# A decoder layer in fp32: single transposes between half units, a shared ring of load buffers, and seven-product units moved within the down projection

## The chip, the cores and the metric

The kernel runs on one core of one Trainium2 chip. The metric is the device time of one execution in microseconds; the median of three runs before the change is 1808.32 us (1804.74 to 1811.37). Five engines work side by side, each through its own queue in order: TensorE (PE, with its weight loads shown as PEld), VectorE (DVE), ScalarE (ACT), GpSimd (POOL) and SyncE (SP), which here issues nearly all transfers from memory.

## The reference

One layer of a decoder for 256 tokens of width 2048, all in float32. Cut to what matters:

```
def swiglu(x, w_gate, w_up, w_down):
    return (jax.nn.silu(x @ w_gate) * (x @ w_up)) @ w_down        # d_ff 5632

x = layer_norm(ALPHA * x + 0.5 * swiglu(x, ffn1_w_gate, ffn1_w_up, ffn1_w_down), ln1_g, ln1_b)
(c_q, c_kv, k_rope, q, k_c, v_c, k_s, v_s, k_w, v_w, g) = split_cols(x @ w_in, IN_SIZES)
o_mla = mla_attention(...)      # 8 heads, low-rank queries and keys
o_nsa = nsa_attention(...)      # 8 heads, compressed, selected and window branches
mix = jnp.concatenate([o_mla, o_nsa], axis=-1) @ w_out
x = layer_norm(ALPHA * x + mix, ln2_g, ln2_b)
x = layer_norm(ALPHA * x + 0.5 * swiglu(x, ffn2_w_gate, ffn2_w_up, ffn2_w_down), ln3_g, ln3_b)
```

The two SwiGLU layers hold most of the matmuls: each reads three matrices of 2048 x 5632.

## The kernel before

**Products.** Every fp32 operand is split into a high part (a cast on ScalarE, L81) and the rest (a subtraction on VectorE, L82), and one product is three matmuls of 512 columns (`mm3`, L86 to L88): high by high, high by low, low by high. The weights are split on the chip, piece by piece, as they arrive.

**Two ways to multiply.** `gemm` takes one chunk of 512 output columns and walks the input in pieces of 256 rows; a piece is one load of 512 KB (`load`) and 12 matmuls, for two halves of the tokens. `gemm2` takes a pair of chunks; a unit is 256 input rows by 1024 columns, two loads, and eight products, 24 matmuls. For the units in a list (`seven`) it uses seven products in place of eight: VectorE makes four sums of weight blocks (L236 to L238, into the tiles `sum`), and sums of the activations must have been made before. Four more banks collect these products, and after the last such unit ScalarE and VectorE make four corner values from them (L254 to L258, in working tiles `w`), to which the ends of the other four banks are added (L266). `GATE7`, `UP7` and `DOWN7` are the lists.

**Order of a SwiGLU layer.** The eleven chunks of d_ff stand in groups of 4, 4 and 3. In a group, pairs of chunks are gated: gate weights, then up weights (`gemm2`, except that the first pair of a layer loads its gate weights by `gemm`). Then the group's rows go through `down`: two pairs of output chunks over the group's input rows. In the third group `down` uses four single chunks. `NW` (10) working tiles hold the gated rows; `NM` (14) tiles `m` hold sums of activations and attention operands.

**Transposes.** A gated row block (128 tokens by 512) has to be transposed for `down`: four transposes into one bank (`go`, L365), then a split into tiles `thi`, `tlo`; where `down` has seven-product units, sums of the rows are transposed too (`go2`, L375). These steps are generators that `spawn` puts in lanes and `tick` advances. TensorE and SP run in the order in which the program is written, and a tick is where a waiting step may put its instructions in. `gemm2` ticks twice after each unit; `gemm` twice after each piece. While a seven-product stretch needs all eight banks, `held` keeps the steps waiting. ScalarE, VectorE and GpSimd are ordered by a scheduler when the program is built.

**Buffers.** Loads go into five tiles `raw`, weight sums into three tiles `sum`, splits into six pairs `whi`, `wlo`; TensorE has eight banks. SP issues loads in order and waits where the next buffer is still in use.

Of the kernel before, what the change touches and what calls it, by code (L numbers as in the profile page):

```python
# [18 lines left out]
P = 128  # L19
# [14 lines left out]
O_CKV, O_KR, O_Q, O_KC, O_KS, O_KW, O_G = 512, 768, 832, 1856, 2368, 2880, 3392  # L34
KT = 2
HEAD, SPARE = 8, 2
NM = 14
NW = 10
GATE7, UP7 = (2, 4, 5), (1, 2, 4, 5)
DOWN7 = (((3, 5), (1, 3, 5)), ((3, 5), (1, 3, 5)), ((), ()))  # L40
DFF, DTR, DEV, DLN, DSM = 4, 7, 2, 4, 4


# [1 line left out]
def layer(ctx: ExitStack, tc: tile.TileContext, a: dict, out: bass.AP):  # L45
# [34 lines left out]
    def split(hi, lo, src):  # L80
        A.copy(hi, src)  # L81
        V.tensor_tensor(lo, src, f(hi), op=OP.subtract)  # L82

    def mm3(ps, x, wh, wl, first, last):
        xh, xl = x
        PE.matmul(ps, xh, wh, start=first, stop=False)  # L86
        PE.matmul(ps, xh, wl, start=False, stop=False)  # L87
        PE.matmul(ps, xl, wh, start=False, stop=last)  # L88
# [28 lines left out]
    def tick(n):  # L117
        for _ in range(n):
            now[0] += 1
            steps()  # L120

    def drain(*which):
        while any(q in lanes for q in which) if which else lanes:
            tick(1)

    def load(w, c, pc, spare=False):

        ap, pairs, n = w[:3]
        paired = len(w) > 3
        k0, kn = pc[0], len(pc)  # L130
        assert pc == list(range(k0, k0 + kn)) and k0 // KT == pc[-1] // KT
        r0 = (c * pairs + k0 // KT) * P
        raw = rawp.tile([P, KT, NCH], F32, name="raw")
        order = list(range(kn))
        if paired:

            r0 = (c // 2 * pairs + k0 // KT) * P
            src = w[3][r0:r0 + P].rearrange("p (i j n) -> p i j n", i=2, j=2)[:, :, c % 2, :]
            if c % 2:
                order = order[::-1]  # L140
            if kn < KT:
                at = k0 % KT if c % 2 == 0 else 1 - k0 % KT
                src = src[:, at:at + 1]
            nc.sync.dma_start(raw[:, :kn, :n], src)
        else:
            nc.sync.dma_start(raw[:, :kn, :n], ap[r0:r0 + P].rearrange("p (k n) -> p k n", k=KT)[:, k0 % KT:k0 % KT + kn])
        if spare:
            out = []
            for j in range(kn):
                hi, lo = (am(F32R).rearrange("p a b -> p (a b)")[:, :n] for _ in range(2))  # L150
                split(hi, lo, raw[:, j, :n])
                out.append((hi, lo))
            return [out[j] for j in order]
        hi = hip.tile([P, KT, NCH], F32R, name="whi")
        lo = lop.tile([P, KT, NCH], F32R, name="wlo")
        split(hi[:, :kn, :n], lo[:, :kn, :n], raw[:, :kn, :n])
        return [(hi[:, j, :n], lo[:, j, :n]) for j in order]
# [46 lines left out]
    def gemm2(x, xs, seven, w, cp, kps, finish, each=None):  # L204

        src, pairs = W2[w]
        B, todo = {}, []
        s_first, s_last = min(seven), max(seven)
        for i in kps:
            k, l = 2 * i, 2 * i + 1
            if i in seven:
                todo.append((i, [("p1", (k, 0), "kn"), ((0, 1), 3, "lm"), ((0, 0), (l, 0), "ln"), ("p5", 0, "t1"),
                                 ("p7", 2, "t3"), ("p6", 1, "t2"), ((1, 0), (l, 1), "t4")]))
            else:
                todo.append((i, [((t, j), (kk, t), name) for name, kk, j in  # L220
                                 (("kn", k, 0), ("lm", l, 1), ("ln", l, 0), ("km", k, 1)) for t in range(NT)]))
        first, last = {}, {}
        for i, ops in todo:
            for o, op in enumerate(ops):
                first.setdefault(op[0], (i, o))
                last[op[0]] = (i, o)
        rest = {}
        for i, ops in todo:
            r0 = (cp * pairs + i) * P
            a_, b_ = (rawp.tile([P, KT, NCH], F32, name="raw") for _ in range(2))  # L230
            for j, dst in enumerate((a_, b_)):
                nc.sync.dma_start(dst, src[r0:r0 + P, 2 * j * NCH:2 * (j + 1) * NCH].rearrange("p (k n) -> p k n", k=KT))
            parts = [(a_, ("kn", "lm"), 2), (b_, ("ln", "km"), 1 if i in seven else 2)]
            if i in seven:
                t13, t24 = (sump.tile([P, KT, NCH], F32, name="sum") for _ in range(2))
                V.tensor_tensor(t13, a_, b_[:, 1:2, :].broadcast_to([P, 2, NCH]), op=OP.add)  # L236
                V.tensor_tensor(t24[:, 0], t13[:, 0], a_[:, 1], op=OP.add)  # L237
                V.tensor_tensor(t24[:, 1], t24[:, 0], b_[:, 0], op=OP.add)  # L238
                parts += [(t13, ("t1", "t3"), 2), (t24, ("t2", "t4"), 2)]
            wt = {}  # L240
            for v, names, n in parts:
                hi = hip.tile([P, KT, NCH], F32R, name="whi")
                lw = lop.tile([P, KT, NCH], F32R, name="wlo")
                split(hi[:, :n], lw[:, :n], v[:, :n])
                for j in range(n):
                    wt[names[j]] = (hi[:, j], lw[:, j])
            for o, (b, xp, name) in enumerate(ops):
                if b not in B:
                    B[b] = new_bank()
                xp = sl(xs[i], xp) if isinstance(xp, int) else x(*xp)  # L250
                mm3(B[b], xp, *wt[name], first[b] == (i, o), last[b] == (i, o))
            if i == s_last:
                p1, q, u, z = (wk([P, NCH]) for _ in range(4))
                A.copy(p1, B["p1"])  # L254
                V.tensor_tensor(q, B["p6"], p1, op=OP.add)
                V.tensor_tensor(u, B["p7"], q, op=OP.add)
                V.tensor_tensor(q, B["p5"], q, op=OP.subtract)
                V.tensor_tensor(z, B["p5"], u, op=OP.subtract)  # L258
                rest = {(0, 0): p1, (0, 1): q, (1, 0): u, (1, 1): z}

            held[0] = s_first - 1 <= i <= s_last
            tick(2)
            if each:
                each(i)
        for b, r in rest.items():
            V.tensor_tensor(r, B[b], r, op=OP.add)  # L266
            finish(*b, r)
# [30 lines left out]

    def load_x(k, n=2):

        raw = rawp.tile([P, KT, NCH], F32, name="raw")
        nc.sync.dma_start(raw[:, :n, :S], a["xT"][k * P:(k + n) * P, :].rearrange("(k p) n -> p k n", p=P))
        for t in range(NT):
            if k % 4 == 0:
                xT[k // 4, t] = new_T()
            hi, lo = xT[k // 4, t]
            j = k % 4
            split(hi[:, j:j + n, :], lo[:, j:j + n, :], raw[:, :n, t * P:(t + 1) * P])
        if k // KT in UP7:
            xs0[k // KT] = parts(sums([raw[:, j, t * P:(t + 1) * P] for t in range(NT) for j in range(2)]))  # L310
# [34 lines left out]
    def ffn(name, x, xs, done, begin=None, after=None, late=()):  # L345
# [4 lines left out]
        for gi, grp in enumerate(groups):  # L350
# [4 lines left out]
            def up(c, t, h):  # L355

                hs[c, t] = h

                def go(c=c, t=t):
                    yield DFF  # L360
                    while held[0]:
                        yield 1
                    pt = new_bank().rearrange("p (a b) -> p a b", a=4)
                    for j in range(4):
                        PE.transpose(pt[:, j, :], hs[c, t][:, j * P:(j + 1) * P], ident)  # L365
                    hT[c, t] = new_T()
                    split(hT[c, t][0], hT[c, t][1], pt)

                def go2(i, s):
                    yield DFF  # L370
                    while held[0]:
                        yield 1
                    pt = new_bank().rearrange("p (a b) -> p a b", a=4)
                    for j in range(4):
                        PE.transpose(pt[:, j, :], s[:, j, :], ident)  # L375
                    hS[i] = parts(pt)

                spawn(go())
                if t:
                    for i in (2 * c, 2 * c + 1):  # L380
                        if i in seven[0] | seven[1]:
                            spawn(go2(i, sums([hs[c, u][:, (2 * (i % 2) + j) * P:(2 * (i % 2) + j + 1) * P]
                                               for u in range(NT) for j in range(2)])))
                steps()

            for c0 in grp[::2]:
# [430 lines left out]
    def compress(src, n):  # L817
# [26 lines left out]
        for m in range(2):  # L844
            PE.transpose(pt[:, m, :], hs[:, m * P:(m + 1) * P], ident)
        hid = att.tile([P, 2, 32], F32, name="hid", bufs=2)
        x = stat.tile([P, 2, 32], F32, name="gx")
        u = stat.tile([P, 2, 32], F32, name="gu")
        V.tensor_reduce(x, pt[:, 0:2, :].rearrange("p m (j c) -> p m c j", j=4), axis=AX.X, op=OP.add)
        V.tensor_tensor(u, x, x, op=OP.mult)  # L850
        V.tensor_tensor(u, u, x, op=OP.mult)
# [209 lines left out]
```

## Time and profile before

| what | value |
|---|---|
| median of three runs | 1808.32 us |
| the profiled execution | 1809.37 us, its span 1807.7 us |
| TensorE busy | 1770.5 us (98%), 8166 matmuls |
| VectorE busy | 1532.3 us (85%) |
| ScalarE busy | 975.7 us (54%) |
| moved by DMA | 350 MB, 194 GB/s over the span |

Times are microseconds from the span's start. The end of a matmul in the trace is modelled, and matmuls overlap, so a busy TensorE says little about its pace; the distance between starts does. A number in square brackets at a row's end is the idle time of the engine just before it and what ended it.

### The profile page before, as it was taken

The numbers are of one execution on the slowest core, as the hardware profiler recorded it, in microseconds if no ns is written. First come the engines' busy times: TensorE is split into PE (matmuls) and PEld (weight loads), VectorE is DVE, ScalarE is ACT, GpSimd is POOL, SyncE is SP. The second block draws the span as 40 slices with busy tenths as digits, with TensorE's granted clock in tenths as the row PEclk, the third lists the DMA queues.
The fourth block names the chain that finished last, engine by engine and source line by source line (L and its number), as shares of the span: only waits on it lengthen the run. The fifth ranks groups of instructions, "written<-read, shape, count | busy, mean of one in ns | idle before, by whom it ended". The sixth has DMA issues, their size and how long they took to land.

```text
span 1807.7 us, 22569 instructions
## 1 busy us (share of the span) xinstructions
PE 1770.5 (98%) x8166; PEld 1454.8 (80%) x8166; DVE 1532.3 (85%) x2019; ACT 975.7 (54%) x1285; POOL 17.4 (1%) x40
## 2 busy tenths in 40 slices
PE   7999999999999999999999999999999999999997
PEld 5887888888888888887787787878888888888886
DVE  6899899999889986766466678899999999889976
ACT  5556455565546554644455556556456565556541
POOL 0000000000000000000000000000000000000000
PEclk9999999999999999999999999999999999999999
DMA  7765565556465665565643445566655655555564
GB/s 252 248 209 195 183 214 201 197 186 207 167 209 203 197 219 191 167 199 194 235 142 117 129 166 170 198 191 206 219 188 202 205 184 202 191 201 204 196 222 139
DMA packets 112543, 350.01 MB, mean 194 GB/s; under 512 B 11168, under 2 KB 17584, under 8 KB 112432
## 3 DMA queue, kind: packets, MB, share of 16 engines
q1 hardware_dynamic: 111120, 344.37, 57.2%
q0 software_dynamic: 1312, 4.21, 0.9%
q8 instruction: 64, 1.05, 0.2%
q14 instruction: 47, 0.39, 0.1%
HBM read 346.44 MB, written 2.10 MB: 193 GB/s over the span
## 4 chain that ended last, share of the span: by engine, by line
PE 86%; DVE 8%; DMA 3%; issue 2%; ACT 2%; SPq 0%; DVEq 0%; POOL 0%; ACTq 0%; POOLq 0%
PE bank L86 27%; PE bank L88 27%; PE bank L87 27%; DVE wlo L82 3%; DMA raw<-in_ffn_w_gate 2%; ACT whi L81 1%; DMA raw<-in_ffn_w_up 1%; PE bank L910 1%; PE bank L365 1%; PE bank L900 1%; PE bank L754 1%; DVE sum L236 1%; DVE w L395 1%; PE bank L836 1%; DVE w L266 1%
## 5 line engine op out<-in xcount | busy, mean ns | idle before, releaser
L81 ACT CAST whi<-raw 128x1024 fp32r<-128x1024 f32 (+3 forms) x622 | 599.3, 982 | 496.3 <-PE bank L88 392.7
L82 DVE TENSOR_TENSOR wlo<-raw,whi 128x1024 fp32r<-128x1024 f32 (+3 forms) x622 | 694.0, 1130 | 153.0 <-ACT whi L81 151.9
L86 PE MATMUL bank<-whi,thi 128*128 128x512 f32 (+1 forms) x2026 | 794.2, 392 | 3.5 <-ACT whi L81 1.8
L87 PE MATMUL bank<-wlo,thi 128*128 128x512 f32 (+1 forms) x2026 | 786.6, 388 | 2.8 <-DVE wlo L82 2.8
L88 PE MATMUL bank<-whi,tlo 128*128 128x512 f32 (+1 forms) x2026 | 786.1, 388 | 0.1
L86 PEld LDWEIGHTS bank<-whi,thi 128*128 128x128 f32 x2026 | 381.2, 188 | 85.2 <-issue 4.5
L87 PEld LDWEIGHTS bank<-wlo,thi 128*128 128x128 f32 x2026 | 381.4, 188 | 79.8 <-DVE wlo L82 5.2
L88 PEld LDWEIGHTS bank<-whi,tlo 128*128 128x128 f32 x2026 | 381.0, 188 | 78.2 <-DVE tlo L82 0.5
L81 ACT CAST whi<-sum 128x1024 fp32r<-128x1024 f32 x184 | 191.5, 1053 | 196.6 <-PE bank L88 78.7
L82 DVE TENSOR_TENSOR wlo<-sum,whi 128x1024 fp32r<-128x1024 f32 x184 | 219.5, 1217 | 15.9 <-ACT whi L81 14.9
L87 PE MATMUL bank<-wlo,m 128*128 128x512 f32 x368 | 143.4, 390 | 1.2 <-DVE wlo L82 1.2
L88 PE MATMUL bank<-whi,m 128*128 128x512 f32 x368 | 143.2, 389 | 0.0
L86 PE MATMUL bank<-whi,m 128*128 128x512 f32 x368 | 143.2, 389 | 0.0
L236 DVE TENSOR_TENSOR sum<-raw 128x1024 f32<-128x1024 f32 x92 | 111.9, 1217 | 17.4 <-DMA raw<-in_ffn_w_gate 15.7
L87 PEld LDWEIGHTS bank<-wlo,m 128*128 128x128 f32 x368 | 69.1, 188 | 16.2 <-DVE wlo L82 2.0
L86 PEld LDWEIGHTS bank<-whi,m 128*128 128x128 f32 x368 | 69.1, 188 | 14.4
L88 PEld LDWEIGHTS bank<-whi,m 128*128 128x128 f32 x368 | 69.1, 188 | 14.3
L266 DVE TENSOR_TENSOR w<-bank,w 128x512 f32<-128x512 f32 x112 | 74.4, 684 | 3.5 <-PE bank L88 3.5
L237 DVE TENSOR_TENSOR sum<-sum,raw 128x512 f32<-128x512 f32 x92 | 62.9, 684 | 0.5
L238 DVE TENSOR_TENSOR sum<-sum,raw 128x512 f32<-128x512 f32 x92 | 62.9, 683 | 0.5
L82 DVE TENSOR_TENSOR tlo<-bank,thi 128x512 fp32r<-128x512 f32 (+1 forms) x56 | 34.0, 642 | 4.0 <-ACT thi L81 4.0
L81 ACT CAST thi<-bank 128x512 fp32r<-128x512 f32 (+1 forms) x56 | 28.6, 558 | 16.2 <-PE bank L365 10.0
(178 smaller groups left out, 880.6 us busy)
## 6 DMA issues: line engine op xcount, KB each, us to landing
raw<-in_ffn_w_down SPq DMA_DIRECT2D x176, 512.0 KB, 4.6
raw<-in_ffn_w_up SPq DMA_DIRECT2D x160, 512.0 KB, 4.8
raw<-in_ffn_w_gate SPq DMA_DIRECT2D x159, 512.0 KB, 4.6
raw<-in_w_in SPq DMA_DIRECT2D x48, 512.0 KB, 4.5
raw<-in_ffn_gu SPq DMA_DIRECT2D x32, 512.0 KB, 5.0
raw<-in_w_out SPq DMA_DIRECT2D x32, 512.0 KB, 3.3
raw<-in_nsa_cmp_w_k SPq DMA_DIRECT2D x8, 512.0 KB, 3.7
raw<-in_nsa_cmp_w_v SPq DMA_DIRECT2D x8, 512.0 KB, 3.4
```

What stands on the lines that cost most here:

```text
L81: A.copy(hi, src)
L82: V.tensor_tensor(lo, src, f(hi), op=OP.subtract)
L86: PE.matmul(ps, xh, wh, start=first, stop=False)
L87: PE.matmul(ps, xh, wl, start=False, stop=False)
L88: PE.matmul(ps, xl, wh, start=False, stop=last)
L236: V.tensor_tensor(t13, a_, b_[:, 1:2, :].broadcast_to([P, 2, NCH]), op=OP.add)
L237: V.tensor_tensor(t24[:, 0], t13[:, 0], a_[:, 1], op=OP.add)
L238: V.tensor_tensor(t24[:, 1], t24[:, 0], b_[:, 0], op=OP.add)
L266: V.tensor_tensor(r, B[b], r, op=OP.add)
L365: PE.transpose(pt[:, j, :], hs[c, t][:, j * P:(j + 1) * P], ident)
L395: V.tensor_tensor(h, r, h, op=OP.mult)
L754: PE.matmul(o, qrT[t][:, hh, :], krT[:, b, :], start=False, stop=True)
```

## The change

Four edits. `go` and `go2` all go into one lane, "T", and take one tick each, so that at most one set of four transposes follows a tick; `gemm2` ticks once in the middle of a unit (after its fourth operation) and once at its end. The lists of `down`: the first chunk pair has no seven-product unit any more and is done by single chunks with `gemm`; the second has the units 1, 2, 4 and 5 (before: 3 and 5, and 1, 3 and 5). Plain loads and the loads of x take their buffer from `new_raw`, which goes round five `raw` and three `sum` tiles. The pools: 16 tiles `m` (14), 9 working tiles (10), two tiles each for `gx` and `gu` (three).

```
-NM = 14
-NW = 10
+NM = 16
+NW = 9
 GATE7, UP7 = (2, 4, 5), (1, 2, 4, 5)
-DOWN7 = (((3, 5), (1, 3, 5)), ((3, 5), (1, 3, 5)), ((), ()))
+DOWN7 = (((), (1, 2, 4, 5)), ((), (1, 2, 4, 5)), ((), ()))
...
+    turn = [0]
+
+    def new_raw():
+
+        turn[0] += 1
+        return (sump if turn[0] % 8 >= 5 else rawp).tile([P, KT, NCH], F32, name="sum" if turn[0] % 8 >= 5 else "raw")
+
     def load(w, c, pc, spare=False):
...
-        raw = rawp.tile([P, KT, NCH], F32, name="raw")
+        raw = new_raw()
...
                 mm3(B[b], xp, *wt[name], first[b] == (i, o), last[b] == (i, o))
+                if o == 3:
+                    tick(1)
...
             held[0] = s_first - 1 <= i <= s_last
-            tick(2)
+            tick(1)
...
+                ready = now[0] + DFF
+
                 def go(c=c, t=t):
-                    yield DFF
-                    while held[0]:
+                    while held[0] or now[0] < ready:
                         yield 1
                     pt = new_bank().rearrange("p (a b) -> p a b", a=4)
                     for j in range(4):
                         PE.transpose(pt[:, j, :], hs[c, t][:, j * P:(j + 1) * P], ident)
                     hT[c, t] = new_T()
                     split(hT[c, t][0], hT[c, t][1], pt)
+                    yield 1
...
-                spawn(go())
+                spawn(go(), "T")
...
                             spawn(go2(i, sums([hs[c, u][:, (2 * (i % 2) + j) * P:(2 * (i % 2) + j + 1) * P]
-                                               for u in range(NT) for j in range(2)])))
+                                               for u in range(NT) for j in range(2)])), "T")
```

`go2` changes as `go` does, and `load_x` as `load`. The change adds lines, so that an instruction's line after it is higher: L365 becomes L375, L375 becomes L385, L258 becomes L267, L266 becomes L275.

On TensorE, in the second gate stage of the first layer, the transposes stand before the change in one place, at the end of the seventh unit:

```order
L86 MATMUL bank<-whi,thi 128x512
L87 MATMUL bank<-wlo,thi 128x512
L88 MATMUL bank<-whi,tlo 128x512
L365 MATMUL bank<-ident,w 128x128 x12
L375 MATMUL bank<-ident,w 128x128 x4
L365 MATMUL bank<-ident,w 128x128 x4
L375 MATMUL bank<-ident,w 128x128 x4
L86 MATMUL bank<-whi,thi 128x512
```

After the change the same place holds the first four, and the next four stand 12 matmuls later (four products of three):

```order
L88 MATMUL bank<-whi,tlo 128x512
L375 MATMUL bank<-ident,w 128x128 x4
L86 MATMUL bank<-whi,thi 128x512
L87 MATMUL bank<-wlo,thi 128x512
L88 MATMUL bank<-whi,tlo 128x512
```

The other sets follow in the same way, one at the end of the stage, one in the first unit of the up stage, and the last two at the up stage's end. In the first down chunk two sets stand together after a piece (x8).

On SP, the first loads of the program, with the semaphores that each waits for; before the change the sixth is the first that waits for VectorE:

```order
L302 DMA raw<-in_xT 128x2x256
L144 DMA raw<-in_ffn_w_gate 128x2x512 [waits DMAHW0_49,DVE_49]
L302 DMA raw<-in_xT 128x2x256 [waits DMAHW1_49,DVE_49]
L144 DMA raw<-in_ffn_w_gate 128x2x512 [waits DMAHW2_49,DVE_49]
L302 DMA raw<-in_xT 128x2x256 [waits DMAHW3_49,DVE_49]
```

After it, from the same load on:

```order
L311 DMA sum<-in_xT 128x2x256
L151 DMA sum<-in_ffn_w_gate 128x2x512
L311 DMA sum<-in_xT 128x2x256
L151 DMA raw<-in_ffn_w_gate 128x2x512
L311 DMA raw<-in_xT 128x2x256 [waits DMAHW0_49,DVE_49]
```

The order of the loads is the same; the ninth is now the first that waits.

On VectorE, the corner values of that gate stage (L255 to L258) and what follows, before the change:

```order
L257 TENSOR_TENSOR w<-bank,w 128x512
L258 TENSOR_TENSOR w<-bank,w 128x512
L236 TENSOR_TENSOR sum<-raw 128x1024
L82 TENSOR_TENSOR wlo<-raw,whi 128x1024
L82 TENSOR_TENSOR tlo<-bank,thi 128x512 x3
L82 TENSOR_TENSOR m<-bank,m 128x512
L82 TENSOR_TENSOR tlo<-bank,thi 128x512
L82 TENSOR_TENSOR m<-bank,m 128x512
```

And after it:

```order
L266 TENSOR_TENSOR w<-bank,w 128x512
L243 TENSOR_TENSOR sum<-raw 128x1024
L82 TENSOR_TENSOR wlo<-raw,whi 128x1024
L267 TENSOR_TENSOR w<-bank,w 128x512
L82 TENSOR_TENSOR tlo<-bank,thi 128x512
L244 TENSOR_TENSOR sum<-sum,raw 128x512
```

The fourth corner value moved behind a weight sum and a weight split, and the splits of the transposed sets no longer stand together.

## Rows read from the trace of the kernel before

**Rows 1.** The page, busy time: engine, us, share of the span, instructions.

```profile
PE 1770.5 (98%) x8166; PEld 1454.8 (80%) x8166; DVE 1532.3 (85%) x2019; ACT 975.7 (54%) x1285; POOL 17.4 (1%) x40
```

**Rows 2.** TensorE's waits: for whom, us in total, times, longest.

```profile
PE bank L365 <- DVE tlo L82: 9.4, 8, 1.9
PE bank L86 <- ACT m L81: 7.4, 2, 5.3
PE bank L87 <- DVE wlo L82: 4.1, 6, 1.2
```

**Rows 3.** Stretches by stage: us, busy PE, PEld, DVE, ACT, POOL, clock, DMA, GB/s.

```profile
100.30:146.80 46.50, 44.55 (x209) 36.89 (x208) 45.78 (x63) 25.57 (x31) 0.00 (x0) 1.00 0.56 183
187.60:233.50 45.90, 44.60 (x208) 37.05 (x207) 40.10 (x51) 22.46 (x26) 0.00 (x0) 1.00 0.54 176
233.50:275.00 41.50, 41.50 (x185) 34.37 (x184) 37.65 (x43) 22.25 (x23) 0.00 (x0) 1.00 0.61 206
357.20:402.70 45.50, 44.61 (x209) 36.92 (x208) 44.97 (x61) 25.70 (x31) 0.00 (x0) 1.00 0.56 187
...
655.70:723.60 67.90, 67.67 (x309) 55.94 (x307) 45.93 (x58) 32.21 (x39) 0.56 (x1) 1.00 0.59 192
...
1174.80:1222.40 47.60, 45.05 (x208) 36.72 (x207) 45.98 (x64) 24.06 (x30) 2.73 (x5) 1.00 0.62 192
1222.40:1263.20 40.80, 40.80 (x181) 33.78 (x180) 40.57 (x46) 25.12 (x29) 0.00 (x0) 1.00 0.62 202
1263.20:1308.50 45.30, 44.60 (x207) 37.03 (x206) 44.99 (x60) 21.89 (x26) 1.62 (x3) 1.00 0.66 222
1432.30:1477.40 45.10, 44.45 (x208) 36.87 (x207) 44.34 (x60) 25.61 (x31) 0.00 (x0) 1.00 0.56 187
```

**Rows 4.** Timeline of TensorE around one burst: start, us, operation, idle before.

```profile
135.21 0.39 PE L87 MATMUL bank<-wlo,thi 128*128 128x512 f32 x1
...
136.12 0.39 PE L88 MATMUL bank<-whi,tlo 128*128 128x512 f32 x1
...
140.20 0.66 PE L365 MATMUL bank<-ident,w 128*128 128x128 f32 x4 [1.95 <-DVE tlo L82]
...
142.00 0.40 PE L86 MATMUL bank<-whi,thi 128*128 128x512 f32 x1
```

**Rows 5.** Timeline of TensorE around a set of four transposes alone.

```profile
718.89 0.39 PE L88 MATMUL bank<-whi,tlo 128*128 128x512 f32 x1
...
720.26 0.40 PE L86 MATMUL bank<-whi,thi 128*128 128x512 f32 x1
```

**Rows 6.** The start: stretches, TensorE's first matmuls and its pause, an SP wait.

```profile
5.30:35.50 30.20, 25.98 (x96) 19.05 (x96) 21.36 (x47) 17.98 (x33) 0.00 (x0) 1.00 0.82 274
35.50:59.50 24.00, 23.76 (x96) 19.29 (x97) 18.20 (x18) 12.83 (x14) 0.00 (x0) 0.93 0.85 292
...
30.00:35.00 5.00, 2.95 (x12) 1.99 (x11) 1.19 (x2) 2.55 (x4) 0.00 (x0) 1.00 1.01 358
35.00:40.00 5.00, 4.26 (x12) 3.20 (x13) 4.04 (x4) 4.87 (x7) 0.00 (x0) 0.74 0.69 234
...
8.30 0.63 PE L86 MATMUL bank<-whi,thi 128*128 128x512 f32 x1
8.73 0.63 PE L87 MATMUL bank<-wlo,thi 128*128 128x512 f32 x1
...
35.51 0.50 PE L86 MATMUL bank<-m,thi 128*128 128x512 f32 x1 [2.17 <-ACT m L81]
...
SPq L144 <- DVE tlo L82: 7.0, 5, 2.8
```

**Rows 7.** Timeline of TensorE at a wait in the stretch from 1174.80.

```profile
1190.69 0.50 PE L87 MATMUL bank<-wlo,m 128*128 128x512 f32 x1 [1.23 <-DVE wlo L82]
```

**Rows 8.** Groups of instructions: count, busy us, mean ns, idle before.

```profile
L375 PE MATMUL bank<-ident,w 128*128 128x128 f32 x48 | 7.4, 277 | 0.0
L258 DVE TENSOR_TENSOR w<-bank,w 128x512 f32<-128x512 f32 x28 | 19.0, 678 | 0.0
```

More of the change, by code (lines that the diff above doesn't have):

```diff
@@ L299, in load_x @@
     def load_x(k, n=2):
-        raw = rawp.tile([P, KT, NCH], F32, name="raw")
+        raw = new_raw()
         nc.sync.dma_start(raw[:, :n, :S], a["xT"][k * P:(k + n) * P, :].rearrange("(k p) n -> p k n", p=P))
@@ L367, in go @@
                     split(hT[c, t][0], hT[c, t][1], pt)
+                    yield 1
                 def go2(i, s):
-                    yield DFF
-                    while held[0]:
+                    while held[0] or now[0] < ready:
                         yield 1
@@ L376, in go2 @@
                     hS[i] = parts(pt)
-                spawn(go())
+                    yield 1
+                spawn(go(), "T")
                 if t:
@@ L846, in compress @@
         hid = att.tile([P, 2, 32], F32, name="hid", bufs=2)
-        x = stat.tile([P, 2, 32], F32, name="gx")
-        u = stat.tile([P, 2, 32], F32, name="gu")
+        x = stat.tile([P, 2, 32], F32, name="gx", bufs=2)
+        u = stat.tile([P, 2, 32], F32, name="gu", bufs=2)
         V.tensor_reduce(x, pt[:, 0:2, :].rearrange("p m (j c) -> p m c j", j=4), axis=AX.X, op=OP.add)
```

## The prediction

> **What bounds the kernel now.** I read the busy shares first. TensorE is busy for 98% of the span, VectorE for 85% [rows 1]: what the kernel can win is in TensorE's pauses and in its count of instructions. Second, the waits of TensorE [rows 2]: the longest sum, 9.4 us in 8 waits, is the transposes of the SwiGLU rows (L365) waiting for the VectorE half of a split (L82), which frees a bank. The second, 7.4 us in 2 waits, is the start of the program, where a split waits for a weight that has not landed.
>
> Third, the stretches stage by stage, cut at the first matmul of each stage [rows 3]. The pitch of a matmul is 0.227 us (four from 135.21 to 136.12 [rows 4]), and a stage of 183 matmuls without transposes lasts 41.50 us = 183 x 0.227: nothing but pitch. Eight stages are longer: four of gate weights (46.50, 45.50, 47.60, 45.10; 183 matmuls each) and four of down's first chunk pair (45.90, 45.30 and two like the first of these; 186 each, so 42.18 without transposes). Together 367.7 us against 4 x 41.50 + 4 x 42.18 = 334.7: 33 us over. 1.5 of it is another wait, in the stretch at 1174.80: 1.23 us for a split that VectorE reaches late [rows 7], with the slower pitch behind it. The other 31.5 us are 176 transposes in eight bursts. In one burst (24 transposes, 136.12 to 142.00) the pause is 1.95 us: the fifth set of four finds no free bank [rows 4].
>
> The start: two stages of 96 matmuls (21.8 us of pitch each) last 30.20 and 24.00 us [rows 6], 10.6 us over.
>
> **The change part by part.**
>
> *One set of transposes per half unit.* It removes the eight bursts. How much does a set of four cost alone? From the matmul at 718.89 to that at 720.26 are 1.37 us, which hold four matmuls (0.91) and one set: 0.46 us [rows 5]. The order after the change has 48 sets in the two groups concerned (44 before; the L375 row counts 12 sums rows in 48 transposes [rows 8], and the new list of units makes 16), with 12 matmuls between most of them and pairs of sets in the first down chunk. 48 x 0.46 = 22.1 us, against 31.5: **-9.4 us**. In the third groups two runs of 16 and 8 become six sets: +0.1 us each, +0.2.
>
> What hides the splits of a set? Each needs a ScalarE and a VectorE pass of about 0.6 us beside 2.7 us of matmuls, and VectorE has room where they now go: the down stages lose work (two seven-product units fewer in the first pair, no corner sums to finish), the gate stages hold three splits in place of six. If that cover were gone, the 9.4 us of waits [rows 2] would come back as waits of single sets. I add **+1.5 us** for sets that come late (the first down chunk has two in a row, and the last gate rows of a layer reach down only 6 matmuls after their transposes); bounds 0 and +9.4.
>
> *Down: first pair plain, second with four units.* Per layer and group 2 + 3 = 5 seven-product units become 4, and each saves 3 matmuls of 24. Two layers, two groups: 4 units fewer, 12 matmuls more, x 0.227 = **+2.7 us**, all on the path. VectorE in the second pair gets one unit more; an up stage with the same four units ran in exactly its pitch, 40.80 us for 180 matmuls, with VectorE at 40.57 [rows 3], so I cost the fourth unit at nothing beyond. The plain loads fetch runs of 2 KB in place of 4 KB. The last down stage already loads so: 67.90 us for 288 matmuls and 20 transposes (65.4 + 2.2), at a DMA share of 0.59 [rows 3]. Nothing added.
>
> Against this stands a rule of the Trainium skill, Perfetto Trace Analysis, section DMA Optimizations: larger transfers fill the memory's bandwidth better, and going from 2 KB to 4 KB or 8 KB can improve throughput dramatically. If halving the run halved the rate, the share of 0.54 in the first-pair stage would pass 1 and the four stages would become transfer-bound, by some 0.08 x 45.9 x 4 = 15 us, 1812. The row of the last down stage, with such runs at 192 GB/s and no wait, disagrees, so that rule gets a chance of 2 in 100.
>
> *Plain loads also use the sum tiles.* At the start SP issues a load only when a buffer comes free: with five, its gate loads wait for VectorE again and again (7.0 us behind one line alone [rows 6]), while in 30 to 35 us the transfers show that they can run at 358 GB/s. With eight, the first eight issues wait for nothing and every later one is three buffers ahead. The first chunk needs 2.1 MB of x and 4.2 MB of weights; at 358 GB/s that is 17.6 us, at the 274 of the stretch 23 us, and TensorE wants the last piece about 25 us in. VectorE needs 21.36 us of work there. So the stage falls from 30.20 to about 24.5: 21.8 of pitch, 2.5 because its first dozen matmuls stand 0.43 us apart as at 8.30 and 8.73 [rows 6] (12 x 0.2), and little else. The wait of 2.17 us at 35.51 goes, and with it the second half of its price: behind that pause the granted clock is 0.74 in the mean of 35 to 40 us, part of it at the lower of its two levels, 1.2 GHz, part at the upper, 2.4. Together up to 5.7 + 2.2 = 7.9 us; the bounds are 0 (transfers or VectorE bind anyway) and 8.2 (all but the cold dozen). I take **-6.0**, nearer to the upper end, since of the three limits only the buffers are at theirs. In the mixer and the other plain stages TensorE hardly waits for loads: 0.
>
> *Pools of 9 work tiles and 16 m tiles, two gx and gu.* Nine working tiles must hold what ten held. The order of VectorE changes for it: the fourth corner value (L258, L267 now) stands two splits later, behind the first set of transposes that frees a tile, and the second residual product is split by a weight split, which brings that split 1.2 us earlier and may shorten the 1.23 us wait [rows 7]. I take 0, bounds -1.2 and +2.
>
> Sum: -9.4 + 0.2 + 1.5 + 2.7 - 6.0 = -11.0 us. It is made against the profiled execution, 1809.4 us with a span of 1807.7, 1 us above the median of 1808.32: 1797.3 for the median.
>
> **The rivals.**
>
> *The start stays as it is* (transfers or VectorE take the place of the buffers). For it: VectorE works 21.36 of the first stage's 30.20 us [rows 6], and TensorE waits 4.1 us for its splits in L87 [rows 2], most of it there. Against: its share of the stage is 71%. 1797.3 + 6.0 = 1803.3.
>
> *The waits move instead of going*: sets come one by one, but their splits queue behind weight splits on VectorE, which is at 45.78 of 46.50 us in a gate stage [rows 3]. Then the 9.4 us stay, in place of 1.5: 1805.2. Against: with a set per 2.7 us each has its own bank.
>
> *Slower: nine working tiles bind.* Between the end of one gated product and the next, four rows, two sum rows and four corner values want ten tiles. If VectorE, which takes its instructions in order, stands at the fourth value until a transposition frees one, all weight splits behind it wait, and TensorE with them once its six split buffers are used up. There are 24 such ends (28 now, L258 [rows 8]). With a loss of one L258, 0.68 us, at each: +16.3, 1813.6, above the time before; it decides from 0.46 us per end on. Against: L258 already runs at the moment of the first set, and the new order puts two splits ahead of it.
>
> **How the numbers follow.** Forecast 0.63; the start stays 0.16; the waits move 0.10; nine tiles 0.06; 2 KB runs 0.02; anything else 0.03. A difference of 0.3%, 5.4 us, is about what a measurement of this kernel can tell from no change, so "faster" means below 1802.9. The forecast lies there but for 0.01; the start rival by half (0.08), the moved waits by 0.04: 0.74 faster. The slower cases give 0.07; the rest, 0.19, is the same. The range: below, all of the start and the shorter wait on top (1797.3 - 2.2 - 1.2 - 1.5 = 1792.4); above, the start rival with another microsecond, and part of the moved waits, to 1804.5.
>
> **What would show it.** Right: L365's wait of 9.4 us is below 3; the gate stages last near 41.5 + 3 x 0.46 us; L86 and L87 count 12 more; the second gate chunk starts near 30 us, with no wait for the m split and a granted clock near 1 in 35 to 40 us. Wrong: waits of the new sets for VectorE above 5 us; a second chunk that starts at 34 us or later; waits of VectorE for the matmuls or transposes just ahead of L267; waits for weights in down's first pair.

## The result and the profile after

The changed kernel takes 1798.27 us (median of 6 runs, 1797.63 to 1801.46), the kernel before 1807.69 us (6 runs, 1804.74 to 1811.37): ratio 0.9950, 95% interval 0.9937 to 0.9964. The profiled execution has a span of 1796.7 us, 11.0 below that of before. 9.4 us were measured between the medians, 11.0 forecast.

The page first, busy time of TensorE by us, share and count, to be held against [rows 1]:

```profile
PE 1772.0 (99%) x8194; PEld 1453.9 (81%) x8194; DVE 1500.6 (84%) x1987; ACT 967.7 (54%) x1277; POOL 17.5 (1%) x40
```

The waits of TensorE after the change, us in total, times, longest:

```profile
PE bank L86 <- ACT m L81: 5.4, 1, 5.4
PE bank L87 <- DVE wlo L82: 2.8, 3, 1.2
...
PE bank L86 <- ACT whi L81: 2.2, 2, 1.8
```

The longest sum of [rows 2], transposes that wait for a split, is gone altogether, and of the 7.4 us for `m` only the program's first wait of 5.4 us is left.

The stretches by stage after the change, cut at the first matmul of each stage as in [rows 3] (us, busy time with count of each engine, clock, DMA share, GB/s). In order: second gate, its up stage, first and second down pair, a gate stage of the second group, last down stage; then gate, up and first down pair of the second SwiGLU layer:

```profile
94.20:137.00 42.80, 42.80 (x195) 35.41 (x194) 41.95 (x56) 22.26 (x26) 0.00 (x0) 1.00 0.55 188
137.00:179.50 42.50, 42.50 (x195) 35.01 (x194) 41.03 (x47) 27.54 (x33) 0.00 (x0) 1.00 0.66 221
179.50:225.80 46.30, 46.30 (x217) 38.49 (x216) 33.87 (x46) 19.33 (x22) 0.00 (x0) 1.00 0.52 180
225.80:266.60 40.80, 40.80 (x181) 33.80 (x180) 36.46 (x40) 23.82 (x25) 0.00 (x0) 1.00 0.58 195
348.90:391.70 42.80, 42.80 (x196) 35.43 (x195) 42.23 (x56) 22.51 (x26) 0.00 (x0) 1.00 0.56 197
645.60:714.70 69.10, 68.75 (x315) 56.26 (x313) 46.64 (x60) 32.93 (x41) 0.56 (x1) 1.00 0.56 194
1164.30:1209.50 45.20, 43.86 (x197) 35.14 (x195) 43.59 (x60) 22.12 (x25) 2.19 (x4) 1.00 0.63 196
1209.50:1252.30 42.80, 42.76 (x194) 34.85 (x193) 42.01 (x49) 27.36 (x33) 0.00 (x0) 1.00 0.63 212
1252.30:1298.90 46.60, 46.56 (x217) 38.40 (x216) 38.96 (x55) 19.33 (x22) 2.16 (x4) 1.00 0.60 198
```

A gate stage with three sets lasts 42.80 us, which is the 41.50 of [rows 3] plus 3 x 0.46 to within 0.1; three more sets now stand in the up stage, which was 40.80. Of the gate stages shown, only the one from 1164.30 is longer than that: by 2.4 us.

Counted over the whole trace (from the starts of the first matmul of every stage, before and after):

| part | before | after | difference |
|---|---|---|---|
| first two gate chunks | 54.2 | 48.1 | -6.2 |
| second gate, its up stage and both down pairs of the first two groups, both layers | 696.8 | 692.4 | -4.4 |
| third groups (their last gate-and-up stage and `down`, with the end of the program) | 230.3 | 231.4 | +1.1 |
| attention part | 361.2 | 359.7 | -1.5 |
| everything else | 465.2 | 465.2 | 0 |

The start, in stretches as in [rows 6]: both stages, the first 10.7 us, and the two stretches about the old pause:

```profile
5.40:31.70 26.30, 25.07 (x97) 18.76 (x98) 22.44 (x48) 19.21 (x34) 0.00 (x0) 1.00 1.00 345
31.70:53.40 21.70, 21.70 (x97) 17.98 (x96) 16.26 (x16) 11.12 (x13) 0.00 (x0) 1.00 0.91 313
5.30:16.00 10.70, 9.42 (x28) 5.84 (x29) 8.34 (x21) 7.31 (x16) 0.00 (x0) 1.00 1.03 351
30.00:35.00 5.00, 5.00 (x24) 4.14 (x23) 2.88 (x4) 4.50 (x6) 0.00 (x0) 1.00 1.04 388
35.00:40.00 5.00, 5.00 (x23) 4.14 (x23) 4.36 (x4) 2.38 (x3) 0.00 (x0) 1.00 0.96 338
```

And from TensorE's timeline the two matmuls of the first stage that still wait longest, with the idle time ahead of each in brackets:

```profile
11.07 0.49 PE L86 MATMUL bank<-whi,thi 128*128 128x512 f32 x1 [0.39 <-ACT whi L81]
12.40 0.50 PE L87 MATMUL bank<-wlo,thi 128*128 128x512 f32 x1 [0.84 <-DVE wlo L82]
```

The second chunk starts at 31.7 us in place of 35.5, without a pause and at full clock, where 35 to 40 us stood at 0.74. The transfers are busy all through the first stage (share 1.00; 0.82 before) and for 0.91 of the second.

The start differs between executions: two traces of this one kernel give 48.1 and 50.3 us for the first two chunks. From the starts of the first matmuls, they last 51.7 to 54.2 us in the four traces of kernels with the old loads (before and runs 2, 3 and 4) and 47.6 to 50.3 us in the nine with a turn of buffers. The means are 4.7 us apart; the -6.2 of the table is one pair of traces.

### The profile page after: what moved, and what is told of

Same layout as the page of the kernel before. It is cut to its first block, busy times and chain, and to the rows that moved or that the text cites. A ratio compares the mean times of both kernels' runs of the same rounds, so it can differ in the third digit from the quotient of the medians.

```text
span 1796.7 us, 22556 instructions
## 1 busy us (share of the span) xinstructions
PE 1772.0 (99%) x8194; PEld 1453.9 (81%) x8194; DVE 1500.6 (84%) x1987; ACT 967.7 (54%) x1277; POOL 17.5 (1%) x40
## 5 line engine op out<-in xcount | busy, mean ns | idle before, releaser
L86 PE MATMUL bank<-whi,thi 128*128 128x512 f32 (+2 forms) x2046 | 805.5, 394 | 3.9 <-ACT whi L81 2.2
L87 PE MATMUL bank<-wlo,thi 128*128 128x512 f32 (+2 forms) x2046 | 793.7, 388 | 2.8 <-DVE wlo L82 2.8
L88 PE MATMUL bank<-whi,tlo 128*128 128x512 f32 (+2 forms) x2046 | 793.9, 388 | 0.2
L81 ACT CAST whi<-raw 128x1024 fp32r<-128x1024 f32 (+2 forms) x533 | 510.4, 975 | 409.2 <-PE bank L88 312.0
L82 DVE TENSOR_TENSOR wlo<-raw,whi 128x1024 fp32r<-128x1024 f32 (+2 forms) x533 | 590.0, 1123 | 101.8 <-ACT whi L81 99.3
L86 PEld LDWEIGHTS bank<-whi,thi 128*128 128x128 f32 x2046 | 384.3, 188 | 86.7 <-issue 5.4
L88 PEld LDWEIGHTS bank<-whi,tlo 128*128 128x128 f32 x2046 | 384.1, 188 | 80.3 <-DVE tlo L82 1.9
L87 PEld LDWEIGHTS bank<-wlo,thi 128*128 128x128 f32 x2046 | 384.6, 188 | 78.6 <-DVE wlo L82 5.0
L81 ACT CAST whi<-sum 128x1024 fp32r<-128x1024 f32 x265 | 274.6, 1047 | 288.4 <-PE bank L88 166.1
L82 DVE TENSOR_TENSOR wlo<-sum,whi 128x1024 fp32r<-128x1024 f32 x265 | 316.1, 1212 | 72.0 <-ACT whi L81 71.8
L87 PE MATMUL bank<-wlo,m 128*128 128x512 f32 x352 | 137.4, 390 | 0.2
L88 PE MATMUL bank<-whi,m 128*128 128x512 f32 x352 | 137.0, 389 | 0.0
L86 PE MATMUL bank<-whi,m 128*128 128x512 f32 x352 | 136.9, 389 | 0.0
L87 PEld LDWEIGHTS bank<-wlo,m 128*128 128x128 f32 x352 | 66.1, 188 | 15.2 <-DVE wlo L82 1.7
L86 PEld LDWEIGHTS bank<-whi,m 128*128 128x128 f32 x352 | 66.1, 188 | 13.9
L88 PEld LDWEIGHTS bank<-whi,m 128*128 128x128 f32 x352 | 66.1, 188 | 13.5
L275 DVE TENSOR_TENSOR w<-bank,w 128x512 f32<-128x512 f32 x96 | 62.6, 681 | 0.0
L660 ACT ACTIVATE w<-w,mx 128x256 f32<-128x256 f32 (+1 forms) x48 | 21.3, 446 | 29.2 <-DVE mx L656 29.2
```

The source lines that it names most:

```text
L660: A.activation(s[:, h, :], s[:, h, :], AF.Exp, bias=mx[:, h:h + 1], accum_out=sm[:, h:h + 1])
```

## The experiments

All times are medians of several runs with runs of the kernel before on the same chip; the ratio is to those.

**1. The turn of buffers alone.** The kernel before, with `new_raw` and, in `load` and `load_x`,

```
-        raw = rawp.tile([P, KT, NCH], F32, name="raw")
+        raw = new_raw()
```

> The kernel before, with the turn over raw and sum tiles for plain loads and nothing else. Theory (the three parts of the change add up): the first stage falls from 30.23 to about 26.3 us, the second from 23.99 to 21.8, nothing else moves: 6.2 us less than before, ratio 0.9966. Rival A (the start gained only together with the rest): under 2 us, ratio above 0.999. Rival B (the 1.5 us that the attention part lost between the two traces belong to the ring): 7.7 us less, ratio 0.9957, and the stretch behind the pause near 896 us shows no slow matmuls in this profile.

Measured: 1803.98 us, ratio 0.9974 (0.9962 to 0.9985). Stretches of its trace: the first gate chunk, one gate stage with a burst, which was 45.50 in [rows 3], and the second gate chunk:

```profile
5.20:31.80 26.60, 25.15 (x97) 18.75 (x98) 22.68 (x48) 19.45 (x34) 0.00 (x0) 1.00 1.01 340
350.60:399.10 48.50, 46.29 (x209) 38.14 (x208) 45.62 (x62) 25.66 (x31) 0.00 (x0) 0.96 0.56 182
31.80:53.50 21.70, 21.70 (x97) 18.00 (x96) 16.35 (x16) 11.34 (x13) 0.00 (x0) 1.00 0.92 319
```

The start falls by 5.9 us in the trace and the time by 4.7 us between the medians; the forecast ratio lies in the interval. Rival A is out, rival B too: the attention part took 362.5 us here, with slow matmuls behind its pause. The middle row shows how a gain is hidden in a single trace: this stage took 3 us more than in the trace of before. Its burst waits 2.2 us in place of 0.9, and behind the wait the granted clock is below full speed (0.96 in the stage's mean).

**2. Everything but the turn.** The kernel after, with `rawp.tile` back in `load` and `load_x`.

> The kernel after, with plain loads from the five raw tiles alone. Theory (parts add up): the start is that of before (30.2 and 24.0 us, with the 2.2 us pause and slow matmuls behind it), the rest that of after: 1798.3 + 6.2 = 1804.5, ratio to before 0.998. Rival (the sets and lists gain nothing by themselves, the whole gain was the ring and chance): 1807.7, ratio 1.000. Rival (the ring costs the down stages something, as they now load plainly): below 1803.5.

Measured: 1805.26 us, ratio 0.9983 (0.9971 to 0.9994), as the first theory has it. The start, at 29.3 and 22.4 us, was 2.5 us shorter in this trace than the theory put it; the pause before the second chunk is there, 1.97 us. The parts add up: 0.9974 x 0.9983 = 0.9957, against 0.9950 for the whole.

**3 and 4. The pools alone; the pools and the list of `down`, with bursts.** Both are the kernel before, with

```
-NM = 14
-NW = 10
+NM = 16
+NW = 9
```

and two `gx` and `gu`; the second with the new `DOWN7` too. (The new list without the new pools, and the old list with single sets, were not run.)

> The kernel before with the pools of after alone: 9 working tiles, 16 m tiles, two gx and gu. Theory (nine tiles do not bind): within 1 us of before, ratio 1.000. Rival (nine tiles bind where VectorE finishes corner values while the transposes stand in bursts): up to 0.68 us at each of 24 ends, 16 us more, ratio 1.009, with TensorE waiting for splits just behind the corner values.

> The kernel before with the pools and the new list of seven-product units of down, but the transposes still in bursts and no turn. Theory (single sets carry the gain): 12 more matmuls cost 2.7 us, the eight bursts hold 24 transposes each (192 in place of 176) and keep their waits of 1 to 2 us, 3 us more: 1807.7 + 5.7 = 1813.4, ratio 1.003. Rival (the lists carry the gain, since the first pair of down no longer ends in corner sums beside the burst): 1804.5 or less, ratio 0.998.

Measured: 1809.25 us, ratio 1.0007 (0.9998 to 1.0015), and 1809.84 us, ratio 1.0008 (0.9999 to 1.0016). Waits in the trace with the pools alone:

```profile
PE bank L365 <- DVE tlo L82: 5.7, 5, 1.3
...
PE bank L375 <- DVE w L258: 3.5, 3, 2.1
```

9.2 us in all, as the 9.4 before. With nine working tiles three bursts wait for a corner value in place of a split, at the same price. The time with the list fell between its theories. Two stretches of its trace, the first down pair and the second gate stage:

```profile
185.80:232.00 46.20, 46.20 (x218) 38.64 (x217) 32.97 (x45) 19.36 (x22) 0.00 (x0) 1.00 0.56 186
98.60:145.00 46.40, 44.64 (x208) 36.88 (x207) 45.34 (x62) 25.65 (x31) 0.00 (x0) 1.00 0.56 182
```

A burst of 24 transposes in the plain down pair costs its pitch and nothing more: 46.20 us, and the single sets of the change take 46.30 there. In the gate stage the burst still waits. In none of the four first down pairs does a transposition wait in this trace; three last 46.2 us, and the fourth, in the second layer, 47.1, with a matmul that waits 0.7 us for a split. So in these stages the list ends the waits, with its plain stage's free banks (it adds up into two at a time) or VectorE's load of 71%, which were not tried apart; in the gate stages it is the single sets. The step from this run to run 2, which is the sets and ticks alone, is 4.6 us.

**5 and 6. Pairs and fours.** The kernel after, with two ticks at the end of a unit and none in its middle; and with four lanes:

```
-                if o == 3:
-                    tick(1)
-            tick(1)
+            tick(2)
```

```
-                spawn(go(), "T")
+                seq[0] += 1
+                spawn(go(), seq[0] % 4)
...
```

(`go2` likewise; `seq` counts the sets of a group.)

> The kernel after, with the step of the lanes twice at the end of a unit in place of once in its middle and once at its end: sets come in pairs every 24 matmuls. Theory (a burst pauses only where it wants a bank that no split has freed; a unit in four products leaves four of eight): pairs cost 0.90 us each, as two singles do, no wait of the transposes, 42.8 and 42.4 us for the gate and up stages of the second group, 1798.3. Rival (VectorE, 95 to 99% busy there, needs the sets one by one): its splits come late by one split of 0.65 us per pair, 14 pairs, 1798.3 + 9 = 1807, the loss seen as waits for transposed or weight splits.

> The kernel after, with the sets spread over four lanes, so that up to four come at one step: 16 transposes, then 8 more 12 matmuls later. Theory (banks): four sets find four banks; the next two come 2.7 us later, when VectorE has had time for about four splits of 0.65 us; waits under 0.5 us per group of sets, gate plus up stage of the second group at most 85.7 us in place of 85.2, 1798 to 1800. Rival (VectorE's order): the next two sets wait 1 us or more in each of the four gate stages as the bursts did (1.3 to 2.3 us), gate plus up 86.5 or more, 1803. In down's first pair, plain with two banks in use, no waits by either.

Measured: pairs 1803.7 us, ratio 0.9971 (0.9961 to 0.9982); fours 1809.06 us, ratio 1.0003 (0.9995 to 1.0012). With pairs, the gate and up stages of the second group and the first down pair of the second layer:

```profile
348.50:391.70 43.20, 43.20 (x201) 35.95 (x199) 42.74 (x59) 22.82 (x26) 0.00 (x0) 1.00 0.58 192
391.70:433.40 41.70, 41.70 (x190) 34.65 (x189) 40.73 (x47) 27.16 (x33) 0.00 (x0) 1.00 0.66 229
1251.10:1302.00 50.90, 48.17 (x218) 39.64 (x217) 39.06 (x53) 19.33 (x22) 2.15 (x4) 0.97 0.59 197
```

Gate plus up is 84.9 us, where single sets take 85.2: pairs fit. The loss sits in one stage, 50.90 in place of 46.60 us. There VectorE comes to the layer norm that is still due, and stands twice for a transfer into a working tile, with the weight splits behind it; TensorE pays (timeline of both engines; L521 is a product of the layer norm):

```profile
1258.30 1.29 DVE L521 TENSOR_TENSOR y<-y,w 128x512 f32<-128x512 f32 x2 [1.27 <-DMA w<-in_ln_g]
...
1262.48 1.29 DVE L521 TENSOR_TENSOR y<-y,w 128x512 f32<-128x512 f32 x2 [1.08 <-DMA w<-in_ln_g]
...
1267.36 0.50 PE L87 MATMUL bank<-wlo,thi 128*128 128x512 f32 x1 [2.73 <-DVE wlo L82]
```

That is 4.3 us of the 5.4 between the medians of pairs and after (3.8 by the ratios, each to its own runs of before). Why VectorE comes to the layer norm ahead of its transfers with pairs, and why the stage did not lose so in the traces with single sets, is not shown. Of the first theory the mechanism held, since no transposition waits for a bank, and the time failed; of the rival the time came nearer, but no pair pays by itself.

With fours, the timeline of TensorE and VectorE about one group of 16 transposes:

```profile
387.05 1.47 PE L376 MATMUL bank<-ident,w 128*128 128x128 f32 x12
390.82 0.66 PE L386 MATMUL bank<-ident,w 128*128 128x128 f32 x4 [2.31 <-DVE w L267]
...
387.82 1.22 DVE L243 TENSOR_TENSOR sum<-raw 128x1024 f32<-128x1024 f32 x1
388.95 1.22 DVE L82 TENSOR_TENSOR wlo<-raw,whi 128x1024 fp32r<-128x1024 f32 x1
390.08 0.68 DVE L267 TENSOR_TENSOR w<-bank,w 128x512 f32<-128x512 f32 x1
```

and the stretch behind it:

```profile
392.00:399.00 7.00, 7.00 (x29) 5.67 (x29) 5.64 (x9) 2.13 (x4) 0.00 (x0) 0.77 0.43 147
```

The fourth set wants the bank that the fourth corner value (L267) still has to read, and L267 stands on VectorE behind a weight sum and a weight split. So only three sets find a bank at once here, not four, and the wait is decided by VectorE's order. It is so in three of the four gate stages (2.1, 2.3 and 0.6 us). With the expectation's two theories: the time is the rival's and worse, the place neither's (the fourth set, not the fifth). Behind the pause the granted clock is 0.77 in the mean of 7 us. The first down pair of the second layer loses here too (53.10 us, with a wait of 4.0 us for a weight split).

**7 and 8. More seven-product units.** The kernel after, with

```
-DOWN7 = (((), (1, 2, 4, 5)), ((), (1, 2, 4, 5)), ((), ()))
+DOWN7 = (((5,), (1, 2, 4, 5)), ((5,), (1, 2, 4, 5)), ((), ()))
```

and the other with `((3,), ())` for the third group as well.

> The kernel after, with one seven-product unit (the sixth) in down's first pair besides the four of the second. Theory (pitch sets the time as VectorE has room there): 12 matmuls less, 12 x 0.227 = 2.7 us, and in that pair single sets in place of pairs with no waits: 1795.6, ratio to before 0.9930. Rival (the corner sums of that pair and the sets bring VectorE's load back to that of before, 99% in one of those stages): the waits eat the 2.7 us, 1798.3 or more.

> As the run with one more unit, and another (the fourth) in the third group's first pair of down chunks: 6 further matmuls less. Theory (pitch): 1795.6 - 1.4 = 1794.2. Rival (the third group's first pair starts with its sets still to come and gemm2 holds more banks): a wait of 1 us or more per layer, 1795.6 or more.

Measured: 1796.94 us, ratio 0.9936 (0.9923 to 0.9948), and 1802.2 us, ratio 0.9962 (0.9949 to 0.9975). With one more, the first two down pairs:

```profile
178.90:224.60 45.70, 45.70 (x214) 37.81 (x213) 37.66 (x52) 21.22 (x25) 0.00 (x0) 1.00 0.53 179
224.60:265.40 40.80, 40.80 (x181) 33.78 (x180) 40.35 (x46) 23.52 (x25) 0.00 (x0) 1.00 0.61 201
```

The first pair falls from 46.30 to 45.70; the second stays at its pitch with VectorE at 99%. With the unit in the third group, both of its down stages:

```profile
644.60:715.10 70.50, 68.79 (x316) 56.13 (x314) 56.57 (x75) 35.06 (x45) 0.56 (x1) 1.00 0.60 204
1719.50:1801.00 81.50, 69.00 (x304) 56.05 (x302) 60.43 (x80) 25.32 (x29) 1.85 (x2) 0.93 0.46 159
```

and the matmuls in them that wait:

```profile
646.28 0.50 PE L86 MATMUL bank<-whi,thi 128*128 128x512 f32 x1 [0.70 <-ACT thi L81]
647.79 0.50 PE L88 MATMUL bank<-whi,tlo 128*128 128x512 f32 x1 [0.77 <-DVE tlo L82]
...
1721.56 0.50 PE L86 MATMUL bank<-whi,thi 128*128 128x512 f32 x1 [1.09 <-ACT thi L81]
1723.07 0.50 PE L88 MATMUL bank<-whi,tlo 128*128 128x512 f32 x1 [0.78 <-DVE tlo L82]
```

Three matmuls fewer, and in the first layer 1.4 us longer than the 69.10 of the change: the first matmuls of the stage now wait for the splits of the sets that come just ahead of them. In the second layer the stage takes 81.50 us in place of 78.07, with slower matmuls behind its waits (clock 0.93 in the mean). Together that is 4.8 of the 5.3 us between the medians of runs 7 and 8. The rival had the wait and its size right; that `gemm2` holds more banks played no part in these rows, which wait for splits.

**9 to 11. Six buffers; after and one more unit side by side.** The first is the kernel after, with `turn[0] % 6 >= 5` for `turn[0] % 8 >= 5`.

> The kernel after, with a turn of six plain loads (five raw, one sum) in place of eight. Theory (with eight the transfers bind in the first 16 us and nothing waits for a buffer any more; the buffers bound with five): six gives back part of the 6.2 us, the first stage between 27 and 29 us, the second 21.8, so 1799 to 1801. Rival (the eighth buffer is not what counts, one more than five already makes the transfers bind): first stage 26.3, 1798.3.

> The kernel after, unchanged, to stand beside the run below on one chip. 1798.3; whether the pause near 887 us (3 us, in every kernel so far) has slow matmuls behind it is chance by my theory, and would be so again if the cause were in the change by the rival (there were none in its first trace).

> The kernel after with the one further seven-product unit in down's first pair, again, beside after itself. Theory: 12 matmuls less, 2.7 us below after, ratio to it 0.9985. Rival (the 1.4 us between the two medians so far were only the other chip, or all there is): the same as after within 1 us.

Measured: 1800.78 us, ratio 0.9962 (0.9948 to 0.9976); after 1798.86 us, 0.9948 (0.9933 to 0.9964); one more unit 1796.88 us, 0.9939 (0.9923 to 0.9955). The first two stages with six:

```profile
4.90:31.40 26.50, 25.18 (x96) 18.65 (x97) 22.11 (x48) 17.48 (x32) 0.00 (x0) 1.00 0.93 309
31.40:53.20 21.80, 21.80 (x97) 18.03 (x97) 16.70 (x16) 13.09 (x15) 0.00 (x0) 1.00 0.95 337
```

My theory of six fell: a turn of six, where a raw tile comes back after six loads in place of five, already gives what eight do, 26.50 and 21.80 us. (Its one sum tile in a turn still goes round all three.) The 1.9 us between its median and that of after, whose ratios overlap in their intervals, are not explained by the start; past the start, its trace had slow matmuls behind two pauses, the trace of after in run 10 behind one. One more unit is the fastest kernel in both of its runs, 1.3 and 2.0 us below after; the four first down pairs of its trace are 2.5 us shorter (12 matmuls fewer), and the intervals of the ratios overlap, so its lead over after is likely and not shown.

## Why the prediction was right, point by point

**The total.** 1797.3 was forecast, 1798.27 measured. That it came out within 1 us is in part luck. Of the 11.0 us between the two traces, 1.5 are the attention part, which takes either time in traces of one and the same kernel (the last section), and the start is 4.7 us shorter in the mean of all traces, not 6.2. With that figure the parts give -4.7 - 4.4 + 1.1 = -8.0 us, 3 less than the sum promised; the measured ratio allows 6.5 to 11.4.

**Single sets (-9.4, and +1.5 for late ones) with the list (+2.7): -5.2 forecast, -4.4 measured.** The price of a set held: three of them in 1.30 us in a gate stage. The waits did go. But the account by edit was wrong in one place: I gave the end of the waits in `down` to the single sets, and run 4 shows that the plain list, with the bursts left in, ends them too. So the list, priced at +2.7, cost 0.6 us more than the pools alone, which the error of both does not tell from nothing.

**The late sets** are real but elsewhere. In the first down pairs hardly any waits. In the third groups, where I put +0.2, the stages of both layers together grew by 1.1: in the first, one set moved from the last gate-and-up stage (42.57 to 42.13) into `down`, 69.10 us in place of 67.90. 0.46 us of that is the set itself, and at 647.81 a matmul that needs its rows starts 0.25 us late, the next 0.11. The other overrun is the gate stage at 1164.30, where VectorE has products of the layer norm to do (L523, L524). The wait of [rows 7] was to shrink by the new order of the splits (0 taken, -1.2 as a bound), and it did: that split now stands ahead of the last of these products, and its matmul, at 1179.04, comes only 0.27 us late. But the next split stands behind that product, which first waits for a transfer, and TensorE waits as long there:

```profile
1177.77 1.22 DVE L82 TENSOR_TENSOR wlo<-sum,whi 128x1024 fp32r<-128x1024 f32 x1
1179.43 1.29 DVE L524 TENSOR_TENSOR y<-y,w 128x512 f32<-128x512 f32 x2 [0.45 <-DMA w<-in_ln_b]
1180.64 2.35 DVE L82 TENSOR_TENSOR wlo<-raw,whi 128x1024 fp32r<-128x1024 f32 x2
...
1181.92 0.50 PE L87 MATMUL bank<-wlo,thi 128*128 128x512 f32 x1 [1.23 <-DVE wlo L82]
```

So the 0 taken was right, though no wait stayed where it was.

**Matmuls.** 12 more, as forecast, but spread over three lines: L86, L87 and L88 have 4 more each (2424 in place of 2420). That "L86 and L87 count 12 more" was a slip.

**The start (-6.0): -6.2 in the two traces, about -4.7 over all of them.** The two parts came out otherwise than argued: the first stage fell to 26.30, not to 24.5, and the second gave back all of its 2.2 us. I had argued that transfers were at 274 of 358 GB/s, so that they would not bind. They do at one place in the first 16 us, which run at 351 GB/s and a share of 1.03: the waits at 11.07 and 12.40. Both come from one weight that ScalarE waits for, and VectorE after it:

```profile
9.97 1.05 ACT L81 CAST whi<-sum 128x1024 fp32r<-128x1024 f32 x1 [0.65 <-DMA sum<-in_ffn_w_gate]
```

Of the stage's 4.5 us over pitch, 2.4 are the first eight matmuls (5.36 to 9.59, forecast at 2.5 for a dozen) and 1.7 these two waits, which the sum did not have. Run 9 has the same two waits at 320 GB/s and a share of 0.94, so what the rows show is the late arrival of this weight, and not that the rate is at its limit. From 16 us on TensorE runs at pitch.

**The rivals.** The start did not stay, the waits did not move to the single sets (no wait of L375 at all). Nine tiles do not bind when the sets come singly; the row of the corner value in the trace after says so with what VectorE waited ahead of it:

```profile
L267 DVE TENSOR_TENSOR w<-bank,w 128x512 f32<-128x512 f32 x24 | 16.3, 681 | 0.7 <-PE bank L375 0.5
```

0.7 us in 24 instructions, where the rival needed 0.46 each. What the late corner value does cost shows with bursts (runs 3, 4 and 6): it holds a bank that the transposes want. The rival of 2 KB runs in the plain down loads is out: 46.30 us at 180 GB/s and a share of 0.52, with no wait for weights. The Trainium skill (Perfetto Trace Analysis, section DMA Optimizations) says that making transfers larger, as from 2 KB to 4 or 8 KB, can improve throughput dramatically, and calls this the primary step when HBM utilization is high but the kernel is DMA-bound. This stage is not bound by transfers, and its trace shows no price for the shorter runs, so the two do not contradict each other.

## What to carry to other kernels

A burst of small work on a full engine can cost a wait beyond its own time; look for the one resource that it takes in number (here banks) and who must free it. In a stage with two banks in use the same burst cost nothing more than its pitch. Before you credit an edit with a wait that went, ask which of the edits alone would have ended it: two here did so in different stages. Small work moved to just ahead of its use brings a wait back (run 8). And a part that differs between executions, like the start here, needs more than one pair of traces.

## What the runs showed of the hardware

The same pause of about 3 us in the attention part (TensorE waits 1.8 us for a cast and 0.8 us for a split) is in all 13 traces. In seven (before and runs 1, 3, 6, 7, 9, 10) matmuls behind it stand 0.43 us apart for some microseconds, in six (after and runs 2, 4, 5, 8, 11) they run at 0.227 at once. The clock granted in the stretch behind it, for the trace of before, of after, and of the after that was run again:

```profile
897.60:903.60 6.00, 6.00 (x22) 4.85 (x23) 3.34 (x3) 2.93 (x5) 0.00 (x0) 0.72 0.76 245
```

```profile
889.00:895.00 6.00, 6.00 (x32) 4.97 (x31) 4.66 (x5) 3.69 (x6) 0.00 (x0) 1.00 1.02 406
```

```profile
891.00:895.00 4.00, 4.00 (x14) 3.08 (x13) 2.92 (x3) 1.10 (x2) 0.00 (x0) 0.61 0.99 383
```

22 matmuls in 6 us against 32: the attention part takes 361.0 to 362.5 us with the fall and 359.6 to 359.7 without. The two traces of after differ in it, and so do the two of one more unit (runs 7 and 11), so one program shows both; what decides between them is not shown. The fall makes this pause dearer than its wait, by 1.3 to 2.9 us in some executions, and it shifts the comparison of two single traces by as much.

At the program's start the granted clock is no help: in the second trace of after it reads 1.00 from 10 to 17 us, although TensorE starts only 15 matmuls in those 7 us:

```profile
10.00:17.00 7.00, 6.48 (x15) 4.56 (x16) 6.70 (x18) 5.83 (x12) 0.00 (x0) 1.00 1.06 371
```

In its first trace full pace began at 9.6 us, in this one at 16.8, and the first stage took 28.5 us in place of 26.3. That is 2.2 us, and the fall in the attention part 1.6, where the two spans, 1800.2 and 1796.7 us, differ by 3.5.
